# Last expert's rows added on chip, first projection weights loaded ahead of the residual, and block norms in two interleaved steps: one change to a two-block transformer kernel

## The chip, the cores and the metric

The kernel runs on one core of one Trainium2 chip. The metric is the device time of one execution in microseconds (us). Before the change three runs took 2792.95, 2793.12 and 2797.24 us; their median is 2793.12 us.

Engine names as the profile has them: PE is TensorE (PEld its weight loads), DVE is VectorE, ACT is ScalarE, POOL is GpSimd, SP is SyncE (here it only issues DMAs).

## The reference, cut to what matters

Two blocks run on 1024 tokens of width 1024. The first ends in a mixture of 16 experts, each of which takes its own 128 of the tokens; a token that several experts chose gets the sum. The second starts with the norm of that sum, the residual, and another norm in front of a wide projection:

```python
y = einsum('becf,efd->becd', silu(hg) * hu, w_down) * g[..., None]
ff = zeros((t, D_MODEL)).at[idx].add(y)
h = h + g2 * rmsnorm(ff, norm_post_ffn)
u = rmsnorm_2(h, norm_w)
proj = einsum('bsd,de->bse', u, w_in)
```

All of it is float32. The kernel keeps that accuracy by writing a number as a high and a low part in a faster format (fp32r) and forming three products, hi*hi, hi*lo and lo*hi (`mm3`). Products of plain fp32 operands appear as two instructions each in the trace.

## The kernel before

**The experts** (`moe`). Expert weights (16 x 12 MB) are read once, in blocks of 256 x 1024 (1 MB). A block lands in one of six `raw` buffers, ACT casts it to the high part `whi`, DVE subtracts to get the low part `wlo` (`split`, L86 and L87), and PE multiplies (`rows`, L766 to L768). The split parts lie in two rings: `mw` (four buffers) takes four blocks of every six, `ml` (two) the others. Step e of the loop forms the gate product `pg` and the up product `pu` of expert e and the down product `py` of expert e-1. ACT makes silu of `pg` (L717), DVE multiplies it with `pu` into `hh` (L718), PE transposes `hh`, and after `py` ACT scales it into `y` (`combine`, L780). POOL then issues an indirect DMA (L781) that adds the 128 rows of `y` to the array `ff_d` in device memory. All sixteen experts go that way.

**The seam** (`block2`, `ffn_out`). For each of eight blocks of 128 tokens SP loads the residual `h` (L808) and `ff` (L810). ACT squares `ff` and sums (L813), two small ACT steps make 1/rms (`rstd`, L91 and L92), DVE scales `ff` (L815) and adds it to `h` (L816), POOL stores `h` (L75, shown as h_d<-h), ACT squares `h` (L818), two more small steps follow, and DVE forms a diagonal matrix `dg` (L821). After four blocks PE multiplies `h` with `dg`, which transposes and scales at once (L827, 64 products in all), and ACT and DVE write the result as high and low part `uh`, `ul` (L829, L830). Then `hgrn` asks for its first projections: `fill(8)` runs two units of the forget gate, two of the query, four of the value (matmuls L81 to L83), whose weights `wk` loads (L840, two `raw` buffers of 4 KB per partition) and splits.

**What sets the order.** The program is unrolled; a scheduler orders each engine's instructions once, when the program is built, and each engine (and each DMA issuing queue) then takes them in that order. A buffer that lies where an older buffer lay waits for that older one. The pool `pj` of the second block begins where the six expert `raw` buffers lay, so its first buffer, the first `raw` of `wk`, takes the place of the ring's slot 0; the buffers of `ffn_out` lie behind, over the last slots and the buffers of `moe`. There are 192 weight blocks (0 to 191) and ahead of them one load of other weights in slot 0, so block 191 lies in slot 0 at the end.

Of the kernel before, what the change touches and what calls it, by code (L numbers as in the profile page):

```python
# [48 lines left out]
class Kernel:  # L49
# [498 lines left out]
    def phase2(self):  # L548

        nc, I = self.nc, self.I  # L550
        with ExitStack() as st:
# [18 lines left out]
            for i in range(8):  # L570
                if i == 4:
                    ple = self.ple_load(w)
# [110 lines left out]
    def moe(self):  # L683

        with ExitStack() as st:
# [3 lines left out]
            pp = self.pool(st, "moep", 1, space=PSUM)  # L689
            xs = self.chosen(0, w, pp)  # L690
            hh = None
            for e in range(NE + 1):
# [82 lines left out]

    def combine(self, e, w, py):

        y = self.t(w, [P, D], F32, "y", bufs=2)
# [5 lines left out]
    def block2(self):  # L784
        with ExitStack() as st:
            self.stu = ExitStack()
            up = self.pool(self.stu, "uT", side="right")
            self.u = [(self.t(up, [P, KB, 512], F32R, f"uh{g}"), self.t(up, [P, KB, 512], F32R, f"ul{g}")) for g in range(2)]
# [3 lines left out]
            with ExitStack() as st2:  # L792
                self.pp = self.pool(st2, "b2p", 2, space=PSUM)
                self.ffn_out()
                self.hgrn()
            self.fox()

    def ffn_out(self):

        nc, pp = self.nc, self.pp  # L800
        with ExitStack() as st:
            w = self.pool(st, "fo")
            for g in range(2):
                us = []
                for b in range(4):
                    r = slice((g * 4 + b) * P, (g * 4 + b + 1) * P)
                    h = self.t(w, [P, D], F32, "h", bufs=8)
                    nc.sync.dma_start(h, self.h_d[r, :])  # L808
                    ff = self.t(w, [P, D], F32, "ff", bufs=4)
                    nc.sync.dma_start(ff, self.ff_d[r, :])  # L810
                    sq = self.t(w, [P, D], F32, "sq", bufs=2)
                    ss = self.t(w, [P, 2], F32, "ss", bufs=4)
                    nc.scalar.activation(sq, ff, AF.Square, accum_out=ss[:, 0:1])  # L813
                    self.rstd(ss[:, 0:1], D)
                    nc.vector.scalar_tensor_tensor(ff, ff, ss[:, 0:1], self.G2, op0=ALU.mult, op1=ALU.mult)  # L815
                    nc.vector.tensor_tensor(h, h, ff, op=ALU.add)  # L816
                    self.store(self.h2_d[r, :], h)
                    nc.scalar.activation(sq, h, AF.Square, accum_out=ss[:, 1:2])  # L818
                    self.rstd(ss[:, 1:2], D)
                    dg = self.t(w, [P, P], F32, "dg", bufs=8)  # L820
                    nc.vector.tensor_scalar(dg, self.ident, ss[:, 1:2], None, op0=ALU.mult)  # L821
                    us.append((h, dg))
                uh, ul = self.u[g]
                for k in range(KB):
                    tp = self.t(pp, [P, 512], F32, "tp", bufs=2)
                    for b, (h, dg) in enumerate(us):
                        nc.tensor.matmul(tp[:, b * P:(b + 1) * P], h[:, k * P:(k + 1) * P], dg, start=True, stop=True)  # L827
                    nw = self.VC[:, 40 + k:41 + k]
                    nc.scalar.activation(uh[:, k, :], tp, AF.Copy, scale=nw)  # L829
                    nc.vector.scalar_tensor_tensor(ul[:, k, :], tp, nw, f(uh[:, k, :]), op0=ALU.mult, op1=ALU.subtract)  # L830
# [716 lines left out]
```

## Time and profile before

| what | value |
|---|---|
| median of three runs | 2793.12 us |
| the profiled execution: its time, its span | 2797.15 us, 2795.4 us |
| PE busy | 2624.6 us (94%), mean granted clock 0.973 |
| DVE, ACT, POOL busy | 71%, 58%, 12% |
| chain that ended last, shares | PE 77%, ACT 7%, DMA 6%, DVE 6%, issue 4% |
| the experts | about 750 to 1331 us, some 36.4 us for each |
| the seam | 1331 to 1395 us |

The span is the time from the first to the last instruction. In the tables of stretches a column such as "4.58 (x16)" is the engine's busy time and the number of its instructions; PEclk is the granted clock of PE, 1.00 being 2.4 GHz and 0.50 being 1.2 GHz. The chain of waits is read from top to bottom: start, length, what the end of the program was then waiting for.

### The profile page before, as it was taken

The numbers are of one execution on the slowest core, as the hardware profiler recorded it, in microseconds if no ns is written. First come the engines' busy times: TensorE is split into PE (matmuls) and PEld (weight loads), VectorE is DVE, ScalarE is ACT, GpSimd is POOL, SyncE is SP. The second block draws the span as 40 slices with busy tenths as digits, with TensorE's granted clock in tenths as the row PEclk, the third lists the DMA queues.
The fourth block names the chain that finished last, engine by engine and source line by source line (L and its number), as shares of the span: only waits on it lengthen the run. The fifth ranks groups of instructions, "written<-read, shape, count | busy, mean of one in ns | idle before, by whom it ended". The sixth has DMA issues, their size and how long they took to land.

```text
span 2795.4 us, 38785 instructions
## 1 busy us (share of the span) xinstructions
PE 2624.6 (94%) x14237; PEld 2207.7 (79%) x14237; DVE 1998.1 (71%) x3298; ACT 1621.1 (58%) x2858; POOL 328.5 (12%) x499
## 2 busy tenths in 40 slices
PE   8999999899699999999599999999999998989998
PEld 5777888777588877777489999998888897778776
DVE  5965899844698888887557767774777776785535
ACT  4213898743477777776535645553666665674335
POOL 0101000000300000000100000001323232330000
PEclk9999999999799999999799999999999999999999
DMA  7666322255599999998622213325675767466612
GB/s 304 199 232 211 95 84 89 82 186 207 202 380 380 371 372 373 374 360 285 234 55 47 46 46 46 46 54 150 176 187 152 180 165 152 144 188 205 188 61 83
DMA packets 294755, 516.45 MB, mean 185 GB/s; under 512 B 52529, under 2 KB 171902, under 8 KB 293540
## 3 DMA queue, kind: packets, MB, share of 16 engines
q1 hardware_dynamic: 267820, 426.67, 48.9%
q0 software_dynamic: 20608, 65.62, 7.1%
q10 hardware_dynamic: 6136, 21.67, 2.0%
q8 instruction: 113, 1.85, 0.3%
q14 instruction: 78, 0.64, 0.1%
HBM read 421.01 MB, written 92.88 MB: 184 GB/s over the span
## 4 chain that ended last, share of the span: by engine, by line
PE 77%; ACT 7%; DMA 6%; DVE 6%; issue 4%; POOL 1%; SPq 0%; DVEq 0%; POOLq 0%; ACTq 0%
PE mm L81 14%; PE mm L83 13%; PE mm L82 13%; PE av L1345 3%; PE pu L767 2%; PE pu L768 2%; PE pu L766 2%; PE pg L767 2%; PE py L768 2%; PE py L767 2%; PE py L766 2%; PE pg L768 2%; PE sc L1307 2%; PE sc L1057 2%; PE tp L1336 2%
## 5 line engine op out<-in xcount | busy, mean ns | idle before, releaser
L87 DVE TENSOR_TENSOR wlo<-raw,whi 128x2048 fp32r<-128x2048 f32 (+1 forms) x280 | 543.5, 1968 | 172.9 <-ACT whi L86 168.8
L86 ACT CAST whi<-raw 128x2048 fp32r<-128x2048 f32 (+1 forms) x284 | 460.0, 1658 | 133.1 <-PE mm L82 59.6
L81 PE MATMUL mm<-uh,whi 128*128 128x512 f32 x640 | 254.7, 398 | 0.9 <-ACT uh L829 0.9
L82 PE MATMUL mm<-ul,whi 128*128 128x512 f32 x640 | 252.6, 395 | 0.0
L83 PE MATMUL mm<-uh,wlo 128*128 128x512 f32 x640 | 251.9, 394 | 0.0
L81 PE MATMUL mm<-whi,uh 128*128 128x256 f32 x768 | 220.3, 287 | 0.0
L83 PE MATMUL mm<-whi,ul 128*128 128x256 f32 x768 | 220.3, 287 | 0.0
L82 PE MATMUL mm<-wlo,uh 128*128 128x256 f32 x768 | 217.9, 284 | 0.0
L83 PEld LDWEIGHTS mm<-whi,ul 128*128 128x128 f32 x768 | 147.1, 192 | 0.1
L81 PEld LDWEIGHTS mm<-whi,uh 128*128 128x128 f32 x768 | 147.0, 191 | 0.1
L82 PEld LDWEIGHTS mm<-wlo,uh 128*128 128x128 f32 x768 | 146.9, 191 | 0.2
L1314 ACT ACTIVATE lg<-lg,sm 128x128 f32<-128x128 f32 (+7 forms) x128 | 99.4, 777 | 81.8 <-DVE sm L1313 81.3
L450 ACT ACTIVATE e<-sc,mx 128x512 f32<-128x512 f32 (+1 forms) x192 | 118.0, 626 | 40.3 <-DVE mx L449 39.5
L83 PEld LDWEIGHTS mm<-uh,wlo 128*128 128x128 f32 x640 | 120.9, 189 | 23.9
L81 PEld LDWEIGHTS mm<-uh,whi 128*128 128x128 f32 x640 | 121.1, 189 | 22.8 <-ACT uh L829 1.4
L82 PEld LDWEIGHTS mm<-ul,whi 128*128 128x128 f32 x640 | 121.2, 189 | 21.5
L81 PE MATMUL mm<-xh,whi 128*128 128x512 f32 x320 | 127.8, 401 | 2.4 <-DVE stl L87 1.4
L82 PE MATMUL mm<-xl,whi 128*128 128x512 f32 x320 | 127.2, 399 | 0.0
L83 PE MATMUL mm<-xh,wlo 128*128 128x512 f32 x320 | 126.7, 397 | 0.5 <-DVE wlo L87 0.5
L1345 PE MATMUL av<-pT,V 128*128 128x256 f32 x640 | 108.5, 299 | 12.5 <-ACT pT L86 11.1
L1345 PEld LDWEIGHTS av<-pT,V 128*128 128x128 f32 x640 | 91.9, 196 | 35.1 <-ACT pT L86 28.4
L449 DVE TENSOR_REDUCE mx<-sc 128x1 f32<-128x512 f32 (+1 forms) x192 | 110.1, 593 | 7.6 <-PE sc L448 6.8
(399 smaller groups left out, 7054.6 us busy)
## 6 DMA issues: line engine op xcount, KB each, us to landing
raw<-in_w_gate_dram SPq DMA_DIRECT2D x64, 1024.0 KB
raw<-in_w_up_dram SPq DMA_DIRECT2D x64, 1024.0 KB
raw<-in_w_down_dram SPq DMA_DIRECT2D x64, 1024.0 KB
raw<-in_w_in_dram SPq DMA_DIRECT2D x76, 512.0 KB
wada<-in_w_ada_dram SPq DMA_DIRECT2D x32, 512.0 KB
Q<-Q_d SPq DMA_DIRECT2D x64, 256.0 KB
yraw<-yT_d SPq DMA_DIRECT2D x22, 512.0 KB
wa<-in_w_ada_dram SPq DMA_DIRECT2D x8, 1024.0 KB
```

The lines of the kernel that those rows point to most:

```text
L81: self.nc.tensor.matmul(ps, ah, bh, start=(i == 0), stop=False)
L82: self.nc.tensor.matmul(ps, ah, bl, start=False, stop=False)
L83: self.nc.tensor.matmul(ps, al, bh, start=False, stop=(i == n - 1))
L86: self.nc.scalar.copy(hi, src)
L87: (eng or self.nc.vector).tensor_tensor(lo, src, f(hi), op=ALU.subtract)
L449: nc.vector.tensor_reduce(mx[:, m, c:c + 1], ps[:, :n], axis=AX.X, op=ALU.min)
L450: nc.scalar.activation(e[:, c0:c0 + n], ps[:, :n], AF.Exp, scale=-1.0, bias=mx[:, m, c:c + 1], accum_out=sm[:, m, c:c + 1])
L766: self.nc.tensor.matmul(ps[n], xh[:, i, :], hi[:, k, c], start=(i == 0), stop=False)
L767: self.nc.tensor.matmul(ps[n], xh[:, i, :], lo[:, k, c], start=False, stop=False)
L768: self.nc.tensor.matmul(ps[n], xl[:, i, :], hi[:, k, c], start=False, stop=(i == KB - 1))
L1314: nc.scalar.activation(lg[:, :n], lg[:, :n], AF.Exp, scale=-1.0, bias=sm[:, 0:1], accum_out=sm[:, 1:2])
L1345: nc.tensor.matmul(ps[:, :256], V[:, k, :], pT[k // 4][j][:, k % 4, :], start=(k + j == 0), stop=(k == nkb - 1 and j == 1))
```

## The change

The last expert's `combine` goes. Its rows stay on chip as `yh` and `yl` (high and low part), and a matrix `oh` of 0 and 1 (from a loaded row 0..1023 and the token numbers, `places`) says which token each row belongs to. In `ffn_out` PE forms for each block identity x `ff` (plain fp32) plus `oh` x `yh` plus `oh` x `yl` in PSUM. ACT squares and DVE scales from PSUM. The norm of a block is in three functions (`first`, `second`, `third`), and the second half of block b follows the first half of block b+1 on ACT. All sixteen loads are written ahead of the norms, each with its own buffer. The first two weight loads of the projections stand ahead of them, and all later ones after the last of them (`issue_after`). The ring of expert `raw` buffers is moved by five slots through five buffers that are never written. `hh`, `sl` and `y` have one buffer in place of two. `uh` and `ul` take buffers of the `mw` ring. The first units run as forget 0, query 0, forget 1, query 1.

```diff
@@ phase2
                 if i == 4:
+                    for _ in range(NR - 1):
+                        self.t(self.rawp, [P, 2, D], F32, "raw")
                     ple = self.ple_load(w)
@@ moe
+            self.stl = ExitStack()
+            lp = self.pool(self.stl, "last", side="right")
+            self.yh, self.yl = [self.t(lp, [P, D], F32R, x) for x in ("yh", "yl")]
+            self.oh = self.t(lp, [P, SEQ], F32R, "oh")
+            self.ix = self.t(lp, [P, 1], F32, "ix")
...
-                    hh = self.t(w, [P, D], F32, "hh", bufs=2)
+                    hh = self.t(w, [P, D], F32, "hh", bufs=1)
                     for n in range(2):
-                        sl = self.t(w, [P, 512], F32, "sl", bufs=2)
+                        sl = self.t(w, [P, 512], F32, "sl", bufs=1)
                         self.silu = self.nc.scalar.activation(sl, pg[n], AF.Silu)
                         self.nc.vector.tensor_tensor(hh[:, n * 512:(n + 1) * 512], sl, pu[n], op=ALU.mult)
-                if e:
+                if e == NE - 1:
+                    self.places(e, w)
+                if e == NE:
+                    gate = self.gT[:, e - 1:e]
+                    for n in range(2):
+                        c = slice(n * 512, (n + 1) * 512)
+                        self.nc.scalar.activation(self.yh[:, c], py[n], AF.Copy, scale=gate)
+                        self.nc.vector.scalar_tensor_tensor(self.yl[:, c], py[n], gate, f(self.yh[:, c]), op0=ALU.mult, op1=ALU.subtract)
+                elif e:
                     self.combine(e - 1, w, py)
-        self.stx.close()
+        self.stu = self.stx
+    def places(self, e, w):
+        nc = self.nc
+        at = self.t(w, [P, D], F32, "xs", bufs=2)
+        nc.sync.dma_start(at, rowbc(self.I["k_iota"]))
+        nc.vector.tensor_copy(self.ix, self.idxT[:, e:e + 1])
+        nc.vector.tensor_scalar(self.oh, at, self.ix, None, op0=ALU.is_equal)
@@ combine
-        y = self.t(w, [P, D], F32, "y", bufs=2)
+        y = self.t(w, [P, D], F32, "y", bufs=1)
@@ block2
-            self.u = [(self.t(up, [P, KB, 512], F32R, f"uh{g}"), self.t(up, [P, KB, 512], F32R, f"ul{g}")) for g in range(2)]
+            self.u = [[[self.t(self.mw, [P, 4, 512], F32R, n) for _ in range(2)] for n in ("whi", "wlo")] for g in range(2)]
...
+                self.lastin = None
+                self.firstw = [self.wk(c0, P) for c0 in (D, 0)]
                 self.ffn_out()
+                self.stl.close()
+                self.pq = self.pool(st2, "b2q", 2, space=PSUM)
                 self.hgrn()
@@ ffn_out
+            pp = self.pool(st, "fop", 1, space=PSUM)
+            sq = self.t(w, [P, D], F32, "sq")
+            hs, ffs = {}, {}
+            def load(to, src, b):
+                to[b] = self.t(w, [P, D], F32, f"in{b // 4}", bufs=8)
+                self.lastin = nc.sync.dma_start(to[b], src[b * P:(b + 1) * P, :])
+            for b in range(4):
+                load(hs, self.h_d, b)
+            for b in range(4):
+                load(ffs, self.ff_d, b)
+            for b in range(4, 8):
+                load(ffs, self.ff_d, b)
+                load(hs, self.h_d, b)
+            def first(b):
...
+                if b in (1, 3):
+                    pss = [(self.t(self.pp, [P, 512], F32, "mm", bufs=3), n * 512, 512) for n in range(2)]
+                else:
+                    pss = [(self.t(pp, [P, D], F32, "ff"), 0, D)]
...
+                for i, (ps, c0, n) in enumerate(pss):
+                    for k in range(0, n, 512):
+                        o, c = ps[:, k:k + 512], slice(c0 + k, c0 + k + 512)
+                        nc.tensor.matmul(o, self.ident, ff[:, c], start=True, stop=False)
+                        nc.tensor.matmul(o, self.oh[:, r], self.yh[:, c], start=False, stop=False)
+                        nc.tensor.matmul(o, self.oh[:, r], self.yl[:, c], start=False, stop=True)
+                    self.sqa = nc.scalar.activation(sq[:, c0:c0 + n], ps, AF.Square, accum_out=ss[:, 2 * i:2 * i + 1])
+            def second(b):
...
+                self.rstd(ss[:, 0:1], D)
+                for ps, c0, n in pss:
+                    nc.vector.scalar_tensor_tensor(ff[:, c0:c0 + n], ps, ss[:, 0:1], self.G2[:, c0:c0 + n], op0=ALU.mult, op1=ALU.mult)
+                nc.vector.tensor_tensor(h, h, ff, op=ALU.add)
+                self.store(self.h2_d[r, :], h)
+            def third(b):
+                pss, dg, ss = state[b]
+                with self.tc.issue_after(self.sqa.ins):
+                    nc.scalar.activation(sq, hs[b], AF.Square, accum_out=ss[:, 1:2])
+                self.rstd(ss[:, 1:2], D)
+                nc.vector.tensor_scalar(dg, self.ident, ss[:, 1:2], None, op0=ALU.mult)
             for g in range(2):
...
+                blks = list(range(g * 4, g * 4 + 4))
+                first(blks[0])
+                second(blks[0])
+                for b in blks:
+                    if b < blks[-1]:
+                        first(b + 1)
+                        second(b + 1)
+                    third(b)
@@ wk
-            nc.sync.dma_start(raw, self.I["w_in_2"][0, r * P:(r + nk) * P, c0:c0 + n].rearrange("(k p) c -> p k c", p=P))
+            with ExitStack() as st:
+                if self.lastin is not None:
+                    st.enter_context(self.tc.issue_after(self.lastin.ins))
+                nc.sync.dma_start(raw, self.I["w_in_2"][0, r * P:(r + nk) * P, c0:c0 + n].rearrange("(k p) c -> p k c", p=P))
@@ hgrn
+            first = [self.jobs.pop(0)[2] for _ in range(2)]
+            self.ready = [(first[j][g], self.firstw[j]) for g in range(2) for j in range(2)]
             self.fill(8)
```

The products of the heads (`sc`, `o`) get a PSUM pool of their own, opened after `ffn_out`.

## Rows read from the trace of the kernel before

**Rows 1.** Stretches around the seam: busy time (instructions) by engine, granted clock, DMA
```profile
1331.00:1355.00 24.00, 0.00 (x0) 0.00 (x0) 7.55 (x7) 9.28 (x19) 2.14 (x2) 0.60 0.91 273
1355.00:1367.00 12.00, 4.58 (x16) 3.71 (x16) 9.28 (x11) 9.96 (x28) 2.19 (x4) 0.50 1.02 405
...
1395.00:1420.00 25.00, 25.00 (x162) 22.85 (x161) 12.93 (x26) 10.27 (x20) 5.66 (x9) 1.00 0.46 126
```

**Rows 2.** The chain of waits through the seam: start us, us, what
```profile
1331.65 10.29 DMA ff_d<-y,idxT
1342.01 5.58 DMA ff<-ff_d
1347.67 1.16 ACT sq L813 x2
...
1366.91 0.68 ACT uh L829
...
1368.43 3.77 PE tp L827 x16
...
1374.17 1.80 PE tp L827 x16
...
1395.48 0.23 PE mm L82
```

**Rows 3.** One stretch, the instructions on tile mm alone (PE's are first)
```profile
1367.00:1395.00 28.00, 12.95 (x42) 8.12 (x43) 0.00 (x0) 0.51 (x1) 0.89 0.38 144
```

**Rows 4.** SP in order of time, 1296 to 1350
```profile
1327.03 11.33 SPq L840 DMA_DIRECT2D raw<-in_w_in_dram  x3
1338.45 0.55 SPq L808 DMA_DIRECT2D h<-h_d  x1
1342.01 0.34 SPq L810 DMA_DIRECT2D ff<-ff_d  x1
```

**Rows 5.** Groups of instructions, 1331 to 1440: count, busy us, mean ns, idle before, releaser
```profile
L827 PE MATMUL tp<-dg,h 128*128 128x128 f32 x128 | 20.9, 319 | 32.8 <-DVE dg L821 32.8
...
L830 DVE SCALAR_TENSOR_TENSOR ul<-tp,VC,uh 128x512 fp32r<-128x512 f32 x16 | 11.6, 747 | 7.6 <-ACT uh L829 7.3
L829 ACT ACTIVATE uh<-tp,VC 128x512 fp32r<-128x512 f32 x16 | 10.8, 686 | 7.0 <-PE tp L827 6.9
L815 DVE SCALAR_TENSOR_TENSOR ff<-ff,ss,G 128x1024 f32<-128x1024 f32 x8 | 10.2, 1279 | 5.3 <-ACT ss L92 5.3
L816 DVE TENSOR_TENSOR h<-h,ff 128x1024 f32<-128x1024 f32 x8 | 9.8, 1221 | 0.1
...
L91 ACT ACTIVATE ss<-ss,epsc 128x1 f32<-128x1 f32 x16 | 4.4, 288 | 0.2
...
L92 ACT ACTIVATE ss<-ss 128x1 f32<-128x1 f32 x16 | 3.0, 196 | 0.2
```

**Rows 6.** The chain of waits near the start, at full clock: plain fp32 products of 512 columns
```profile
26.04 7.82 PE mm L207 x18
```

**Rows 7.** The chain of waits in the last expert's gate and up products
```profile
1294.14 1.28 ACT L1473
1295.43 1.93 ACT whi L86
1297.38 2.30 DVE wlo L87
```

**Rows 8.** All engines in order of time, 1327 to 1350
```profile
1324.72 2.29 DVE L87 TENSOR_TENSOR wlo<-raw,whi 128x2048 fp32r<-128x2048 f32 x1
...
1330.26 0.39 PE L768 MATMUL py<-whi,htl 128*128 128x512 f32 x1
```

**Rows 9.** ACT within one expert's step, in order of time
```profile
1131.54 0.69 ACT L780 ACTIVATE y<-py,gT 128x512 f32<-128x512 f32 x1 [7.43 <-PE py L768]
```

**Rows 10.** DVE within the same step, in order of time
```profile
1119.72 1.37 DVE L718 TENSOR_TENSOR hh<-sl,pu 128x512 f32<-128x512 f32 x2 [1.07 <-PE pu L768]
```

**Rows 11.** The stretch of one expert: busy time by engine, clock, DMA share, GB/s
```profile
1108.00:1144.00 36.00, 34.56 (x160) 28.27 (x159) 30.08 (x19) 26.31 (x20) 3.15 (x2) 1.00 1.01 375
```

More of the change, by code (lines that the diff above doesn't have):

```diff
@@ L798, in ffn_out @@
     def ffn_out(self):
-        nc, pp = self.nc, self.pp
+        nc = self.nc
         with ExitStack() as st:
             w = self.pool(st, "fo")
-            for g in range(2):
[L804 to L823, printed above, removed]
@@ new lines, in ffn_out @@
+            state = {}
+            def first(b):
+                r = slice(b * P, (b + 1) * P)
+                ff = ffs[b]
+                if b in (1, 3):
+                    pss = [(self.t(self.pp, [P, 512], F32, "mm", bufs=3), n * 512, 512) for n in range(2)]
+                else:
+                    pss = [(self.t(pp, [P, D], F32, "ff"), 0, D)]
+                dg = self.t(w, [P, P], F32, "dg", bufs=8)
+                ss = self.t(w, [P, 4], F32, "ss", bufs=4)
+                for i, (ps, c0, n) in enumerate(pss):
[5 more added lines that the diff above has]
+                    self.sqa = nc.scalar.activation(sq[:, c0:c0 + n], ps, AF.Square, accum_out=ss[:, 2 * i:2 * i + 1])
+                state[b] = (pss, dg, ss)
@@ new lines, in second @@
+            def second(b):
+                r = slice(b * P, (b + 1) * P)
+                h, ff = hs[b], ffs[b]
+                pss, dg, ss = state[b]
+                if len(pss) > 1:
+                    nc.vector.tensor_tensor(ss[:, 0:1], ss[:, 0:1], ss[:, 2:3], op=ALU.add)
+                self.rstd(ss[:, 0:1], D)
[3 more added lines that the diff above has]
+                self.store(self.h2_d[r, :], h)
@@ L824, in ffn_out @@
                 for k in range(KB):
-                    tp = self.t(pp, [P, 512], F32, "tp", bufs=2)
-                    for b, (h, dg) in enumerate(us):
-                        nc.tensor.matmul(tp[:, b * P:(b + 1) * P], h[:, k * P:(k + 1) * P], dg, start=True, stop=True)
+                    uh, ul = self.uk(g, k)
+                    tp = self.t(self.pp, [P, 512], F32, "tp", bufs=2)
+                    for i, b in enumerate(blks):
+                        nc.tensor.matmul(tp[:, i * P:(i + 1) * P], hs[b][:, k * P:(k + 1) * P], state[b][1], start=True, stop=True)
@@ L828, in ffn_out @@
                     nw = self.VC[:, 40 + k:41 + k]
-                    nc.scalar.activation(uh[:, k, :], tp, AF.Copy, scale=nw)
-                    nc.vector.scalar_tensor_tensor(ul[:, k, :], tp, nw, f(uh[:, k, :]), op0=ALU.mult, op1=ALU.subtract)
+                    nc.scalar.activation(uh, tp, AF.Copy, scale=nw)
+                    nc.vector.scalar_tensor_tensor(ul, tp, nw, f(uh), op0=ALU.mult, op1=ALU.subtract)
     def wk(self, c0, n):
@@ L866, in prep, with uk @@
             self.ready += [(u, ws) for u in units]
+    def uk(self, g, k, c=slice(None)):
+        return [x[k // 4][:, k % 4, c] for x in self.u[g]]
     def chan(self, ws, g, m=P):
         ps = self.t(self.pp, [P, 512], F32, "mm", bufs=self.nmm)
-        x = self.u[g]
-        self.mm3(ps[:m, :], [(ws[k], (x[0][:, k, :], x[1][:, k, :])) for k in range(KB)])
+        self.mm3(ps[:m, :], [(ws[k], self.uk(g, k)) for k in range(KB)])
         return ps
@@ L878, in toks @@
         for j in range(2):
-            x, t0 = self.u[(b + j) // 4], ((b + j) % 4) * P
-            self.mm3(ps[:, j * 256:(j + 1) * 256], [((x[0][:, k, t0:t0 + P], x[1][:, k, t0:t0 + P]), ws[k]) for k in range(KB)])
+            g, t0 = (b + j) // 4, ((b + j) % 4) * P
+            self.mm3(ps[:, j * 256:(j + 1) * 256], [(self.uk(g, k, slice(t0, t0 + P)), ws[k]) for k in range(KB)])
         return ps.rearrange("p (b c) -> p b c", b=2)
@@ L1053, in product @@
         def product(lv, half, halves, cols, kl, ql):
-            ps = self.t(pp, [P, 512], F32, "sc", bufs=2)
+            ps = self.t(self.pq, [P, 512], F32, "sc", bufs=2)
             pair = lambda ap, c: ap.rearrange("p (a c j) -> p a c j", a=2, c=4)[:, :, c, :]
@@ L1076, in hgrn_head @@
         for c0 in range(0, 8, 4):
-            ps = self.t(pp, [P, 512], F32, "sc", bufs=2)
+            ps = self.t(self.pq, [P, 512], F32, "sc", bufs=2)
             for c in range(4):
@@ L1107, in hgrn_head @@
             n = min(4, 7 - c0)
-            ps = self.t(pp, [P, 512], F32, "sc", bufs=2)
+            ps = self.t(self.pq, [P, 512], F32, "sc", bufs=2)
             for c in range(n):
@@ L1125, in hgrn_head @@
         for c0 in range(0, 8, 4):
-            ps = self.t(pp, [P, 512], F32, "o", bufs=1)
+            ps = self.t(self.pq, [P, 512], F32, "o", bufs=1)
             for c in range(4):
@@ L1517, in shape_constants @@
         "k_ident": np.eye(P, dtype=np.float32),
+        "k_iota": np.arange(SEQ, dtype=np.float32)[None, :],
         "k_cos": np.ascontiguousarray(np.concatenate([cos, cos], 0)),
```

3 lines of the change are left out of this document (1 added, 2 removed).

## The prediction

> **What bounds the kernel now.** I read the stretches first. In the experts the DMA engines are never free (share 1.01, 375 GB/s) while PE works 34.6 of 36 us [rows 11]: both are near their limit, ACT and DVE are not. After the experts PE does nothing for 24 us and little for 12 more, at half clock, and from 1395 it is never idle again [rows 1]. So time can be won between 1331 and 1395, and what PE does later only moves with it.
>
> The chain of waits through this seam says what PE is waiting for. The last product ends at 1330.65 [rows 8]; the last expert's scatter-add takes 10.29 us until it has landed, the first `ff` load behind it 5.58, then the first square starts at 1347.67 and the first `uh` comes at 1366.91 [rows 2]. SP shows a second obstacle: three weight loads stand ahead of the first `h` load and hold SP from 1327.03 to 1338 [rows 4]; the third needs a buffer of the first, which must land and be split.
>
> I count what PE has to do in those 64.4 us (1330.65 to 1395). It is 64 transposing products, 128 instructions, 16 of which take 1.80 at full clock [rows 2, 5], so 14.4 us, and 42 projection products [rows 3] of 0.23 [rows 2], 9.6 us. That is 24.0 us of work, and **40.4 us are lost**. The rest of the text asks what is lost afterwards.
>
> **The change part by part.**
>
> *Work added to PE.* Each block gets two plain fp32 products of 512 columns and four fp32r ones. Eighteen instructions of the plain kind take 7.82 us [rows 6], 0.434 each, two for a product; the fp32r ones take 0.23. So a block costs 4 x 0.434 + 4 x 0.23 = 2.66 us, eight cost 21.2. PE's work in the seam becomes 45.2 us.
>
> *Scatter-add removed.* The 10.29 us leave the chain. In their place ACT writes `yh` as it wrote `y` and DVE writes `yl`, two instructions of the kind of `ul`, 0.75 each [rows 5]: the last ends about 1.5 us after the last product, at 1332.2. `oh` is a DVE instruction of the size of L816, 1.22 us; its cover is DVE's time between the last split (ends 1327.0) and the last product [rows 8]. Without that cover it costs 0 to 1.2 us. Its source is one DMA on SP behind the last expert weights.
>
> By the row this transfer is worth 10.29 us. The Trainium skill, "DMA: Bandwidth & Descriptors", section "Anatomy of one DMA - SWDGE (gpsimd) path", fits about 2.0 us plus bytes over 436 GB/s for a DMA issued there, which would be an estimate of 3.2 us for these 512 KB; the gain below would then shrink by 7 us and turn into a small loss. The row times the very transfer that goes, so I take the row.
>
> *Loads.* With the ring moved by five, slot 0 holds block 186 at the end and slot 5 block 191. The first two weight loads therefore start when 186 is split, well before 1327, and the third no longer stands ahead of the residual. The first two `h` buffers now lie on slot 5: they wait for the last split, at 1327.0 [rows 8]. SP issues four `h` loads, then four `ff` loads; the scatter-add of the last expert but one, on which `ff` waits, is long out by then if it takes what the last one took. The nearest row for a load is the first `ff`, 5.58 us with others in flight [rows 2]. Four loads of 512 KB ahead at the 405 GB/s of [rows 1] are 1.3 us each. From 1327.0, some 2 us for four issues at 0.55 [rows 4], and about 6.6 us for five loads one behind the other: the first `ff` lands near **1335.6**. Bounds: 1330, if the loads whose buffers are free earlier are put ahead, to 1340, if all wait for the last product. PE then loses 5.0 us (0 to 9) before its first block. The stores stay on POOL, whose queue has lost an indirect DMA.
>
> *First four blocks.* ACT per block has two squares of 1.16 [rows 2] and four small steps of 0.29 and 0.20 [rows 5], 3.3 us, 4 with hand-overs. The first square to the first `uh` took 19.2 us before [rows 2]; now first half and second half interleave and I work out 18: one rung of 1.16 + 0.5 + 1.28 + 1.22 + 1.16 + 0.5 us, three more at 4, a transpose. In these 18 us PE has blocks 1 to 3 (8.0), the first of the second four (2.7) and early transposes (1.8): 12.5 us of work, **5.5 lost** (4 to 8).
>
> *Second four blocks.* All use one PSUM tile of two banks, so a block's products wait until DVE has read the block before: a rung is 1.16 + 0.5 + 1.28 + 2.66 and some 0.5 for hand-overs, 6.1 us, four rungs 24.4, then 2.5 for the last second half. PE's filling is the first transposes (7.2), two units that need only the first half (24 products each, 11.0; before, one) and the remaining blocks (8.0): 26.2 us. The rest of the loss is the eight groups of `uh`, `ul` (0.69 and 0.75 [rows 5]) against 0.9 of transposes each. Together **5 lost** (2 to 8).
>
> *Tail of the experts.* ACT loads a function table behind the last silu, 1.28 us, then casts, DVE splits, and PE waits on that [rows 7]. With one `sl` buffer the second silu comes only after the first `hh` product, and the table load with it, out of this path: 1.3 us won. Bounds: the casts of the first weights may stand in front of the last blocks' (each 128x1024, half of the 1.93 and 2.30 of [rows 7]), 2 us lost; or 2 won.
>
> *Edits at nothing.* One `y` and one `hh` buffer: the earlier content is read one step (36 us) before, and even the slowest scatter-add shown takes 10.29. The new order of the units and the PSUM pool of the heads: PE has filled time after 1395 [rows 1]. One `sl` buffer in the other experts: ACT then waits for the first `hh` product (0.69 [rows 10]), but stands idle 7.43 us later in the same step [rows 9].
>
> *Sum.* 45.2 of work and 5.0 + 5.5 + 5 lost are 60.7 us against 64.4: 3.7 won, and 1.3 in the tail, **5.0 us**. The sum is made in the profiled execution (2797.15, span 2795.4), 4.0 above the median of the runs; I take the difference off the median: 2793.1 - 5.0 = **2788.1**.
>
> **The rivals.**
>
> *Loads come early* (chance 0.14). If the scheduler puts the loads with free buffers first, `ff` is there when `yl` is: 1.5 lost in place of 5.0, and 4 and 3 on the ladders. 53.7 us, with the tail a gain of 12: 2781. For it: nothing in [rows 4] but program order forbids it. Against: there the first `h` load came late.
>
> *PE falls to half clock and stays there* (0.18). At 0.50 the clock is granted when PE is busy 4.58 of 12 us [rows 1], and the same 16 instructions take 3.77 in place of 1.80 [rows 2]. The new blocks come in groups with waits between them. If the first four run at 1.2 GHz, the first costs 2.7 more and each further rung 5.3 in place of 4, 6.6 in all, and the gain is eaten: 2794. The Trainium skill, "TensorE: Matmul & The Clock Gate", section "A second HAM failure mode: psum-queue depth-cycling", describes this: short waits for PSUM between groups throw the clock back again and again. The rows agree that sparse groups here ran at half clock; none shows groups as dense as the new ones, 2.7 of 4 us. The same time comes out if the ring shift does not free the weight buffers early, so that they again load ahead of the residual.
>
> *Slower through ScalarE in every expert* (0.13). With one `sl` buffer the second silu waits on ACT until the up product is done, and the casts of the next weight blocks are queued behind it; DVE's second `hh` product and the splits follow late. Per expert that is at most about 0.69 + 0.69 us on the way to PE; 15 times, 20 us, less the 5 won: 2808. For it: PE has only 1.4 us to spare in 36 [rows 11]. Against: the wait of 7.43 us shows ACT ahead of PE [rows 9]. It decides as soon as a cast behind the silu is the one that PE is waiting for.
>
> **How the numbers follow.** Runs of this kernel scatter by about 0.15%, so 0.2% (5.6 us) is what can be told from no change. My forecast has 0.55, with a range of its own from 2780 to 2793 by the bounds above, not all at once: 0.33 of it lies below 2787.5, 0.22 within. Early loads are faster, 0.14. Half clock is the same, 0.16, or slower, 0.02. ScalarE is slower, 0.13. Faster 0.47, same 0.38, slower 0.15. The range is 2778 to 2798: it takes in the early loads and the half clock and leaves out the third rival and the far ends of the bounds.
>
> **What would show it.** Right: no scatter-add after 1320, the first weight casts before the last product, first `h` load near the end of the last split, first square 9 to 10 us after the last product, first `uh` near 28 after it, PE gapless from 61 us after it. Wrong: a first square before 5 us or after 13; clock 0.50 through the first four blocks; PE waiting in the second four for more than 5; or the step of one expert longer than 36.4 us, which would make all of the seam beside the point.

## The result, and the profile after

The change makes the kernel **slower**: 2816.8 us, median of four runs (2812.9 to 2821.6), against 2795.2 for the kernel before beside them (2793.0 to 2798.0). The ratio is 1.0073, 95% interval 1.0061 to 1.0085; 2788.1 was predicted, with a range from 2778 to 2798. The profiled execution took 2818.0 us with a span of 2816.2, 20.8 more than before.

Four marks divide the two spans: the first gate product, the last expert product, and the first scores of head 0 (the first product on `sc` behind the seam).

| stretch | before, us | after, us | difference |
|---|---|---|---|
| start to first gate product | 750.2 | 751.1 | +0.9 |
| experts, to the end of the last product | 580.5 | 575.8 | -4.7 |
| last product to first scores | 111.2 | 129.6 | +18.4 |
| first scores to the end | 1353.5 | 1359.7 | +6.2 |

So the experts gained, and the seam lost much more than that. The third stretch in one row of the table of stretches, for the kernel before and after (columns as in [rows 1]: us, busy time and instructions of PE, PEld, DVE, ACT, POOL; granted clock, DMA share, GB/s):

```profile
1330.65:1441.86 111.21, 77.47 (x468) 64.17 (x469) 54.17 (x75) 53.81 (x114) 12.83 (x19) 0.83 0.55 178
```
```profile
1326.85:1456.48 129.63, 100.76 (x533) 76.07 (x532) 58.82 (x81) 54.34 (x118) 11.14 (x18) 0.87 0.45 149
```

PE has 23.3 us more to do and its idle time falls only from 33.7 to 28.9. Where the 28.9 lie, the waits of PE in the kernel after show (us in total, times, longest):

```profile
PE ff L858 <- DMA in<-ff_d: 17.7, 1, 17.7
PE tp L896 <- DVE dg L881: 8.5, 3, 3.8
PE ff L858 <- DVE in L872: 2.0, 1, 2.0
```

One wait of **17.7 us for the first `ff`** makes up most of it, where 5.0 had been predicted. The chain of waits of the kernel after leads to it (start us, us, what):

```profile
1321.00 0.66 DVE oh L797
1321.66 2.21 DVE wlo L87
1323.89 0.37 SPq L912
...
1324.93 2.98 SPq L834
...
1328.01 2.05 SPq L834
1330.11 2.06 SPq L834
...
1332.22 2.26 SPq L834
...
1334.53 9.89 DMA in<-ff_d
...
1344.55 2.04 PE ff L858 x2
```

The weight loads (L912) start at 1323.89, where the last split ends (1321.66 + 2.21 and a hand-over). They stand ahead of the residual and need what the last split frees: just as before ([rows 4], 1327.03 behind a split that ended at 1327.01). The four `h` issues behind them (L834) take 2 us each in place of 0.55 [rows 4], so the first `ff` is issued only at 1334.53, and it lands 9.89 us later, among the loads issued before it. While the `h` loads are being issued, from 1325 to 1334.5, the DMA engines are busy for 0.70 of the time and move 185 GB/s:

```profile
1325.00:1334.50 9.50, 1.85 (x9) 1.20 (x7) 1.61 (x3) 2.35 (x3) 0.00 (x0) 0.70 0.70 185
1334.50:1344.40 9.90, 0.00 (x0) 0.00 (x0) 2.25 (x2) 1.04 (x1) 0.00 (x0) 0.50 0.97 342
```

The other stretches of the kernel after, which answer to [rows 1]:

```profile
1344.50:1350.00 5.50, 5.45 (x9) 2.89 (x10) 0.00 (x0) 0.20 (x1) 0.00 (x0) 0.56 1.03 422
1350.00:1367.00 17.00, 12.25 (x44) 7.07 (x42) 11.79 (x16) 12.46 (x35) 2.26 (x4) 0.98 0.69 269
1367.00:1395.00 28.00, 25.75 (x122) 19.27 (x123) 13.71 (x18) 15.02 (x36) 1.60 (x3) 0.89 0.33 114
1395.00:1407.00 12.00, 7.83 (x33) 6.07 (x32) 6.10 (x6) 4.32 (x12) 3.48 (x5) 0.73 0.11 45
1407.00:1430.00 23.00, 23.00 (x153) 21.05 (x152) 15.08 (x29) 11.66 (x20) 3.19 (x5) 0.99 0.33 89
```

The first block runs at half clock (0.56), as does part of 1395 to 1407, behind a wait of 3.8 us. At half clock the first block's eight instructions last from 1344.55 to 1349.76, 5.2 us; one at full clock (the last) takes 2.9.

### The profile page after: what moved, and what is told of

It is laid out like the page before. It is cut to its first block, busy times and chain, and to the rows that moved or that the text cites. A ratio compares the mean times of both kernels' runs of the same rounds, so it can differ in the third digit from the quotient of the medians.

```text
span 2816.2 us, 38971 instructions
## 1 busy us (share of the span) xinstructions
PE 2645.6 (94%) x14301; PEld 2218.0 (79%) x14301; DVE 2005.9 (71%) x3306; ACT 1619.7 (58%) x2862; POOL 326.0 (12%) x498
## 4 chain that ended last, share of the span: by engine, by line
PE 58%; ACT 5%; issue 3%; DVE 3%; DMA 3%; POOL 1%; SPq 0%; DVEq 0%; POOLq 0%; ACTq 0%
PE mm L81 10%; PE mm L82 10%; PE mm L83 10%; PE av L1423 3%; PE pu L783 2%; PE pu L782 2%; PE pu L781 2%; PE pg L782 2%; PE sc L1385 2%; PE pg L783 2%; PE py L783 2%; PE py L782 2%; PE py L781 2%; PE tp L1414 2%; PE sc L1135 2%
## 5 line engine op out<-in xcount | busy, mean ns | idle before, releaser
L86 ACT CAST whi<-raw 128x2048 fp32r<-128x2048 f32 (+1 forms) x284 | 459.4, 1656 | 121.8 <-PE mm L82 60.0
L81 PE MATMUL mm<-whi,whi 128*128 128x256 f32 (+1 forms) x1408 | 476.7, 339 | 1.5 <-ACT yo L1223 0.8
L83 PE MATMUL mm<-whi,wlo 128*128 128x256 f32 (+1 forms) x1408 | 472.9, 336 | 0.0
L82 PE MATMUL mm<-wlo,whi 128*128 128x256 f32 (+1 forms) x1408 | 470.9, 334 | 0.0
L83 PEld LDWEIGHTS mm<-whi,wlo 128*128 128x128 f32 x1408 | 268.5, 191 | 24.3
L81 PEld LDWEIGHTS mm<-whi,whi 128*128 128x128 f32 x1408 | 268.8, 191 | 24.0 <-ACT whi L898 1.3
L82 PEld LDWEIGHTS mm<-wlo,whi 128*128 128x128 f32 x1408 | 268.6, 191 | 21.7
L450 ACT ACTIVATE e<-sc,mx 128x512 f32<-128x512 f32 (+1 forms) x192 | 117.8, 624 | 40.4 <-DVE mx L449 39.6
L782 PE MATMUL pg<-wlo,xsh 128*128 128x512 f32 x256 | 101.3, 396 | 10.0 <-DVE wlo L87 10.0
L87 DVE TENSOR_TENSOR pT<-tp,pT 128x512 fp32r<-128x512 f32 (+1 forms) x192 | 102.2, 549 | 10.3 <-ACT pT L86 9.4
L1385 PE MATMUL sc<-K,Q 128*128 128x512 f32 (+2 forms) x384 | 101.0, 374 | 6.1 <-DVE lg L1390 6.1
L781 PE MATMUL pg<-whi,xsh 128*128 128x512 f32 x256 | 99.2, 399 | 4.9 <-ACT whi L86 3.8
```

The lines of the kernel that those rows point to most:

```text
L81: self.nc.tensor.matmul(ps, ah, bh, start=(i == 0), stop=False)
L82: self.nc.tensor.matmul(ps, ah, bl, start=False, stop=False)
L83: self.nc.tensor.matmul(ps, al, bh, start=False, stop=(i == n - 1))
L86: self.nc.scalar.copy(hi, src)
L87: (eng or self.nc.vector).tensor_tensor(lo, src, f(hi), op=ALU.subtract)
L450: nc.scalar.activation(e[:, c0:c0 + n], ps[:, :n], AF.Exp, scale=-1.0, bias=mx[:, m, c:c + 1], accum_out=sm[:, m, c:c + 1])
```

## The experiments

Three theories stood against each other. **Entry**: the seam begins late, because the ring was not moved and the slow weight loads go ahead of the residual. **Ladder**: the products added to PE, and the PSUM they hold, are the price wherever the loads are. **Expert**: the single buffers of `hh`, `sl` and `y` cost something in each expert. The kernel before took 2797 to 2799 us beside these runs, and 2795 beside the change, so ratios are compared; 0.1% is 2.8 us. All kernels compute the whole reference.

**Run 1, the ring really moved.** No instruction of the change touches its five extra buffers.

```diff
 for _ in range(NR - 1):
-    self.t(self.rawp, [P, 2, D], F32, "raw")
+    self.nc.gpsimd.memset(self.t(self.rawp, [P, 2, D], F32, "raw")[0:1, 0, 0:1], 0.0)
```

> Each of the five extra ring buffers gets one element written by GpSimd, so that the ring is really moved by five slots. Entry theory (the loss of the change lies where the seam begins: the two weight loads wait for the last split, and the residual waits behind them): the first weight loads are issued before 1315 in place of 1323.9, the first ff lands 5 to 9 us after the last product in place of 17.6, and the time falls 8 to 12 us below that of the change, to 2805 to 2809 us. Ladder theory (the price is the products added to TensorE and the PSUM they hold, wherever the loads are): the first ff is early, but the time stays within 4 us of the change's, 2813 to 2821. Expert theory (single buffers of silu cost something in every expert): the step of an expert and the time stay as with the change.

Measured: 2801.7 us, ratio 1.0022 (1.0012 to 1.0031), by the ratios some 14 us below the change. SP in order of time, PE's waits, and the third stretch of this run:

```profile
1305.36 3.09 SPq L912 DMA_DIRECT2D raw<-in_w_in_dram  x2
1316.66 1.76 SPq L834 DMA_DIRECT2D in<-h_d  x4
1321.83 2.79 SPq L834 DMA_DIRECT2D in<-ff_d  x5
```
```profile
PE ff L858 <- DMA in<-ff_d: 5.4, 1, 5.4
```
```profile
1322.49:1438.96 116.47, 99.83 (x533) 75.45 (x532) 58.58 (x81) 54.17 (x118) 11.19 (x18) 0.93 0.43 146
```

The weights are issued at 1305.36, 17.1 us ahead of the last product instead of 3.0, and the wait for `ff` falls from 17.7 to 5.4. Touching the buffers is the only difference, so in the change the five untouched buffers had taken no place in the ring. The other waits of PE are the same to 0.1 us. Entry holds; but this run is still 0.22% slower than before, so entry is not all. What is left of the wait has another cause, as the chain of waits shows:

```profile
1310.10 11.72 DMA ff_d<-y,idxT
1321.83 5.92 DMA in<-ff_d
```

The first `ff` load waits for the scatter-add of the last expert but one, which here runs beside the early weight loads and takes 11.72 us.

**Run 2, the residual ahead of the weights**, with the ring as in the change.

```diff
-                self.firstw = [self.wk(c0, P) for c0 in (D, 0)]
                 self.ffn_out()
 ...
+            self.firstw = [self.wk(c0, P) for c0 in (D, 0)]
             state = {}
```

> The two weight loads stand behind the residual's sixteen loads instead of ahead of them; all else is as in the change. Entry theory: the first ff lands within 5 us of the last product (17.6 with the change) and TensorE starts its first block 10 to 15 us sooner; the first projections start no later than with the change, as their weights have 20 us and more to come in; time 2802 to 2807 us, 10 to 15 below the change. Ladder theory: the blocks start sooner but the end of the seam moves by less than 4 us, 2813 to 2821 us. Expert theory: no difference, 2816 us.

Measured: 2801.6 us, ratio 1.0017 (1.0008 to 1.0027). PE waits only 1.0 us for its first block, but a later wait grows: 8.3 us in one piece, against 3.3 at that place with the change. The chain of waits says for what:

```profile
1324.47 4.57 DMA in<-h_d
1329.06 19.39 DMA raw<-in_w_in_dram
1348.47 1.04 ACT whi L86
1349.52 1.06 ACT sq L879 x2
```

The cast of the late weights (L86) stands in ACT's queue ahead of a square of the norms (L879) and holds it up. The entry theory expected 10 to 15 us and the profile shows 13.6 of 18.4 won back; the weights are now what comes late.

**Run 3, VectorE in place of the identity product.** Loads as in the change.

```diff
-                        nc.tensor.matmul(o, self.ident, ff[:, c], start=True, stop=False)
-                        nc.tensor.matmul(o, self.oh[:, r], self.yh[:, c], start=False, stop=False)
+                        nc.tensor.matmul(o, self.oh[:, r], self.yh[:, c], start=True, stop=False)
 ...
-                    self.sqa = nc.scalar.activation(sq[:, c0:c0 + n], ps, AF.Square, accum_out=ss[:, 2 * i:2 * i + 1])
+                    nc.vector.tensor_tensor(ff[:, c0:c0 + n], ff[:, c0:c0 + n], ps, op=ALU.add)
+                self.sqa = nc.scalar.activation(sq, ff, AF.Square, accum_out=ss[:, 0:1])
```

> The identity product is taken off TensorE: PSUM holds only the last expert's rows, VectorE adds them to ff in place, ScalarE squares ff from its own buffer. The loads stay as in the change. This removes 8 x 4 x 0.434 = 13.9 us of TensorE's work and frees PSUM after one VectorE step of about 1.3 us. Entry theory: the first ff still lands 17 to 18 us after the last product; of the 13.9 us half comes back, 2807 to 2812 us. Ladder theory: all of it and the stalls of the second four blocks come back, 14 to 20 us, 2797 to 2803. Expert theory: what TensorE saves is won but the 18 us lost in the experts stay, 2803 to 2812.

Measured: 2800.9 us, ratio 1.0011 (1.0002 to 1.0020). PE's longest waits and the third stretch:

```profile
PE ff L858 <- DVE in L860: 20.0, 4, 16.3
PE tp L893 <- DVE dg L878: 5.8, 3, 2.2
```
```profile
1326.30:1442.09 115.79, 87.28 (x500) 69.26 (x500) 67.16 (x87) 54.23 (x114) 11.19 (x18) 0.87 0.50 167
```

The entry wait is still there (16.3 us in one piece, now behind DVE's addition, which waits for `ff`), and PE's idle time is what it was, 28.5. PE has 13.5 us less to do, and all of that is won: 13.8 us of the stretch. The entry theory had expected half, the ladder theory all of it and some stalls besides; the time lies in the ladder theory's range. So PE's added work is a price of its own, beside the entry.

**Run 4, the single buffers alone**, in the kernel before.

```diff
-                    hh = self.t(w, [P, D], F32, "hh", bufs=2)
+                    hh = self.t(w, [P, D], F32, "hh", bufs=1)
 ...
-                        sl = self.t(w, [P, 512], F32, "sl", bufs=2)
+                        sl = self.t(w, [P, 512], F32, "sl", bufs=1)
 ...
-        y = self.t(w, [P, D], F32, "y", bufs=2)
+        y = self.t(w, [P, D], F32, "y", bufs=1)
```

> The kernel before with one buffer for each of hh, sl and y, and nothing else of the change. Expert theory: the step of an expert grows from 36.4 by 0.7 to 1.4 us and the time by 10 to 20 us, to 2805 to 2815. Entry and ladder theories: ScalarE's wait for the first hh product shows (about 2.6 us in each expert) but the step stays within 0.1 us of 36.45, and the time within 3 us of the kernel before.

Measured: 2793.4 us, ratio 0.9988 (0.9979 to 0.9997): a little faster. ACT in the last expert's gate and up products, in order of time (in brackets the idle time before, and its releaser):

```profile
1285.66 0.60 ACT L717 ACTIVATE sl<-pg 128x512 f32<-128x512 f32 x1 [2.54 <-PE pg L768]
1286.15 7.34 ACT L86 CAST whi<-raw 128x2048 fp32r<-128x2048 f32 x4
1297.32 0.60 ACT L717 ACTIVATE sl<-pg 128x512 f32<-128x512 f32 x1 [3.83 <-DVE hh L718]
1297.94 1.28 ACT L1473 ACT_TABLE_LOAD   x1
1299.23 3.72 ACT L86 CAST whi<-raw 128x2048 fp32r<-128x2048 f32 x2
```

ACT does wait for the `hh` product, 3.83 us, but it has cast four weight blocks first, and the steps of the down product in the middle of the experts stay at 36.5 us. The last of these steps falls from 38.8 to 36.5 us, since the table load of [rows 7] is now behind those casts, and the first step of the gate product from 28.2 to 25.8; what shortens that one isn't shown. The experts take 576.4 us in place of 580.5: the expert theory falls, with the sign turned round.

**Run 5, the edits of runs 2 and 3 together.**

```diff
+            self.firstw = [self.wk(c0, P) for c0 in (D, 0)]
             state = {}
 ...
+                    nc.vector.tensor_tensor(ff[:, c0:c0 + n], ff[:, c0:c0 + n], ps, op=ALU.add)
```

> The edits of the second and the third run together: the residual ahead of the weight loads, and VectorE instead of the identity product adding ff. If the entry and TensorE's added work are two separate costs, each of about 15 us, they nearly add up: the way from the last product to the first head's scores (129.6 us with the change, 116.0 and 115.8 with one edit each) falls to 103 to 108 us and the time to 2788 to 2794. If they are one cost seen twice (the same idle time is filled by either), it stays at 113 to 117 us and 2799 to 2803.

Measured: 2787.8 us, ratio **0.9962** (0.9948 to 0.9975), the lowest of all runs, below both kernels. The third stretch is 27.6 us shorter than with the change (13.6 and 13.8 with one edit each):

```profile
1325.40:1427.39 101.99, 87.09 (x501) 69.80 (x501) 65.76 (x87) 53.98 (x114) 11.26 (x18) 0.92 0.49 155
```

Two costs, then, that add up.

**Run 6, the edits of runs 1 and 3 together.**

```diff
+    self.nc.gpsimd.memset(self.t(self.rawp, [P, 2, D], F32, "raw")[0:1, 0, 0:1], 0.0)
 ...
+                    nc.vector.tensor_tensor(ff[:, c0:c0 + n], ff[:, c0:c0 + n], ps, op=ALU.add)
```

> The moved ring (first run) and VectorE instead of the identity product (third run) together. Two separate costs: 102 to 108 us from the last product to the first scores, and 2787 to 2794 us; better than the fifth run by up to 4 us, since the weights are split before the norms and ScalarE doesn't wait for them between two squares. One cost seen twice: 113 to 117 us, 2798 to 2803. If VectorE, with one more step of about 1.2 us per block, becomes what the first four blocks wait for, the first uh comes later than the 29.8 us after the last product of the first run, 32 to 34.

Measured: 2788.3 us, ratio 0.9971 (0.9961 to 0.9981); 102.8 us in the stretch, first `uh` 27.8 us behind the last product. The same as run 5 within the intervals, by the other way of clearing the entry.

**Run 7, the identity product in the first four blocks only.**

```diff
+                        if b < 4:
+                            nc.tensor.matmul(o, self.ident, ff[:, c], start=True, stop=False)
 ...
+                    if b >= 4:
+                        nc.vector.tensor_tensor(ff[:, c0:c0 + n], ff[:, c0:c0 + n], ps, op=ALU.add)
```

> As the sixth run, but the identity product stays in the first four blocks, where TensorE waits anyway, and VectorE adds in the second four only, where TensorE has the transposes and the first projections to do. If TensorE's work counts only where it has no idle time, this is as good as the sixth run or better, by 0 to 4 us; if VectorE isn't the limit in the first four blocks, it is 3 to 6 us slower than the sixth (four identity products of 1.74 us more).

Measured: 2794.3 us, ratio 0.9990 (0.9980 to 1.0001). Some 5 us behind run 6, and 109.4 us in the stretch: products in the first four blocks are not free although PE has idle time there. The first square comes 9.9 us behind the last product in place of 5.8, because a block's products now start only when `ff` is there, and at half clock.

**Run 8, the scatter-add kept**, the rest as in run 1.

```diff
-                if e == NE - 1:
-                    self.places(e, w)
-                if e == NE:
 ...
-                elif e:
+                if e:
                     self.combine(e - 1, w, py)
 ...
+                pss = [(ff, 0, D)]
```

> As the first run (moved ring), but the last expert's rows go out with the scatter-add as before the change, and no products are formed in the norms; ScalarE squares ff from its own buffer. This undoes the on-chip addition alone. If it pays (10.3 us of transfer against products that fit into idle time), this run is 4 to 10 us slower than the first run, 2806 to 2812. If it costs more than it brings (21 us of products against the transfer of 10 us and a load of 6), this run is 5 to 12 us faster than the first, 2790 to 2797 us, with the first square 16 to 18 us after the last product as in the kernel before.

Measured: 2792.3 us, ratio 0.9985 (0.9976 to 0.9994), 0.37% faster than run 1. Its chain of waits:

```profile
1323.40 6.39 DMA ff_d<-y,idxT
1329.81 3.21 DMA in<-ff_d
...
1333.05 1.16 ACT sq L845 x2
```

The first square was expected at 16 to 18 us behind the last product and comes at 10.6. **The scatter-add takes 6.39 us, not the 10.29 of [rows 2]**, and the load behind it 3.21, not 5.58, now that no weight load is issued beside them. So the addition on chip, as the change does it, costs about 10 us more than the transfer that it saves. Done as in run 6, with VectorE in place of the identity product, it does not: run 6 is some 4 us below this run, with a stretch of 102.8 us against 109.3, though the two intervals overlap a little.

**Run 9, the edits of runs 1, 2 and 3 together.**

```diff
+    self.nc.gpsimd.memset(self.t(self.rawp, [P, 2, D], F32, "raw")[0:1, 0, 0:1], 0.0)
 ...
+            self.firstw = [self.wk(c0, P) for c0 in (D, 0)]
 ...
+                    nc.vector.tensor_tensor(ff[:, c0:c0 + n], ff[:, c0:c0 + n], ps, op=ALU.add)
```

> The moved ring, the residual ahead of the weights, and VectorE's addition, all three: a candidate for the best. If the late weights still held ScalarE in the fifth run, they now come earlier and it gains 1 to 4 us on the fifth run: 99 to 102 us from the last product to the first scores, 2784 to 2788 us. If the two entry edits remove the same wait, it is the same as the fifth run within 2 us, 2786 to 2790.

Measured: 2793.4 us, ratio 0.9979 (0.9968 to 0.9991), and 106.9 us in the stretch: a miss. With the ring moved, the first `h` loads are issued at 1318.02 in place of 1306.07 in run 5, and the weights behind the residual at 1332.92 in place of 1329.12. So the weights are on the chain of waits for longer than in run 2, and hold a cast until 1354.4:

```profile
1323.88 10.27 DMA in<-h_d
1334.17 20.25 DMA raw<-in_w_in_dram
1354.44 1.05 ACT whi L86
```

**Run 10, TensorE kept busy**, in run 5.

```diff
+                if b < 4:
+                    dm = self.t(pp, [P, 512], F32, "dm")
+                    for _ in range(8):
+                        nc.tensor.matmul(dm, self.oh[:, r], self.yh[:, 0:512], start=True, stop=True)
```

> The fifth run with eight products of 128x512 (0.23 us each at full clock) into a PSUM tile that nobody reads, behind each of the first four blocks' products, to keep TensorE at full clock through the first four blocks. If half clock there costs (the rival of the prediction), the first transposes and projections run at full clock and the first scores come 2 to 5 us earlier than in the fifth run, 2783 to 2786 us. If ScalarE and VectorE set the pace there and TensorE only waits, nothing is won: 2786 to 2791 us, the first uh at 25 us after the last product as in the fifth run.

Measured: 2794.2 us, ratio 0.9982 (0.9973 to 0.9992). It decides nothing: from 1335 to 1350 the granted clock is 0.74 in place of 0.61, and the first `uh` comes at 31.8 us, later, not sooner; but the chain of waits here also passes through a weight load that lands at 1361.4 and holds ScalarE, so that the part of the added products can't be told from that of the loads.

**Run 11, the loads alone**, in the kernel of run 4.

```diff
-                    nc.sync.dma_start(ff, self.ff_d[r, :])
+                    self.lastin = nc.sync.dma_start(ff, self.ff_d[r, :]) if g * 4 + b < 4 else (nc.sync.dma_start(ff, self.ff_d[r, :]), self.lastin)[1]
 ...
+            with self.tc.issue_after(self.lastin.ins):
```

> The kernel before with one buffer for each of hh, sl and y (fourth run) and with all weight loads of the projections behind the residual's loads, as the only change to the seam; the scatter-add and the norms stay as they were. If the weight loads ahead of the residual were a cost of their own in the kernel before, the scatter-add and the first ff land sooner than 16 us after the last product, the first square comes 4 to 6 us earlier than the 16.8 us of the fourth run, and the time is 2787 to 2790 us. If the scatter-add's own 10.3 us end last whatever SP does, the first square stays at 16 to 17 us and the time within 2 us of the fourth run, 2791.5 to 2795.5. If the weights then come too late, it is slower than the fourth run by 2 to 6 us.

Measured: 2796.1 us, ratio 0.9990 (0.9980 to 0.9999), no gain on run 4. Both halves of the expectation are in its chain of waits:

```profile
1321.67 6.61 DMA ff_d<-y,idxT
...
1329.26 5.75 DMA ff<-ff_d
1335.10 1.15 ACT sq L813 x2
...
1347.64 15.38 DMA raw<-in_w_in_dram
1363.04 1.05 ACT whi L86
```

The scatter-add is again short (6.61, against 10.37 in run 4) and the first square comes at 11.0 us in place of 16.8. Then the weights come late, at 1363, and hold the first projection, where PE waits 4.6 us; the stretch is 112.7 us against 110.3 in run 4.

**Run 12, TensorE kept busy**, in run 6.

```diff
+                if b < 4:
+                    dm = self.t(pp, [P, 512], F32, "dm")
+                    for _ in range(8):
+                        nc.tensor.matmul(dm, self.oh[:, r], self.yh[:, 0:512], start=True, stop=True)
```

> The eight unread products per block again, for the first four blocks, now in the sixth run, where the weights are on chip early and no cast waits for them among the norms (that wait spoilt the tenth run). TensorE's granted clock from the first block to the fourth, 0.58 in the sixth run, should rise to 0.8 or more. If half clock is a price there, the first uh comes before the 27.8 us after the last product of the sixth run and the first scores by 2 to 5 us before its 102.8: 2783 to 2786 us. If ScalarE and VectorE set the pace in the first four blocks, the first uh stays at 27 to 29 us and the time within 2 us of the sixth run, 2786 to 2791.

Measured: 2795.0 us, ratio 0.9986 (0.9976 to 0.9996), slower than run 6 and outside both expectations, with 106.1 us from the last product to the first scores. The stretch of the first blocks in run 6, and in this run:

```profile
1329.00:1350.00 21.00, 12.16 (x34) 8.21 (x34) 17.55 (x21) 14.46 (x37) 2.25 (x4) 0.58 0.95 356
```
```profile
1329.00:1350.00 21.00, 15.06 (x59) 11.22 (x58) 16.63 (x19) 10.75 (x28) 1.73 (x3) 0.81 1.00 384
```

The clock rises from 0.58 to 0.81 as it should, and the first `uh` comes at 30.6 us, not sooner than the 27.8 of run 6: the added products stand in the way of the next block's (the first product of the third block comes 10.9 us behind the last expert product, 5.8 in run 6). So no gain from the higher clock shows, but the run doesn't show either that half clock is free there. DVE is busy 17.6 of 21 us in run 6, which speaks for DVE setting the pace; neither run 10 nor this one decides it. For the change itself, where PE's products stand between `ff` and the square, the question stays open too.

## Why the prediction was wrong

The forecast made the lost time of the seam 5.0 + 5.5 + 5 = 15.5 us beside 45.2 of work. Counted the same way from the table above, the change lost 64.4 + 18.4 - 45.2 = 37.6.

- **The step "Loads" failed.** It said that the first weight loads start well before 1327 because the ring is moved by five, so that the first `ff` costs PE 5.0 us. The ring had not moved, the loads started at the last split, and PE waited 17.7: 12.7 us of the miss. Run 1, with the ring moved, gives 5.4, a first square 10.2 us behind the last product and a first `uh` 29.8 behind it (5.0, 9 to 10 and 28 in the forecast; 17.7, 22.9 and 42.9 with the change). The prediction did name this failure, and the late first square as its sign, but priced it at 6 us, beside the clock's rival: it left out that the weights hold up the residual's issue and its transfer too. Nor was the scatter-add of the last expert but one "long out by then": in run 1 it lands at 1321.83, only 0.7 us ahead of the last product, and the first `ff` load waits for it.
- **Work was priced at full clock, and slow work counted as lost time.** PE's other idle time in the seam is 28.9 - 17.7 = 11.2 us, where 5.5 + 5 had been predicted: the two ladders were right in sum. But 37.6 - 28.9 = **8.7 us** are products that ran slower than priced, most of them at half clock; the forecast had none. In run 1 the same three terms are 5.4, 11.2 and 7.8 us. Little of the 8.7 is new, as PE's waits in the kernel before show:

```profile
PE tp L827 <- DVE dg L821: 32.8, 5, 24.6
PE mm L81 <- ACT uh L829: 0.9, 2, 0.6
```

Of the 40.4 us that the prediction called lost, PE waited only 33.7. The other 6.6 were products: they took 30.6 us in place of the 24.0 priced, at half clock until 1373, and the forecast let these 6.6 us vanish without saying why. The change added 23.3 us of busy time where 21.2 had been priced, so 2.1 of the 8.7 are its own. The rival of half clock did not come as described: it had the first four blocks at 1.2 GHz, for 6.6 us, but only the first was (5.2 us in place of 2.9); the stretch from 1350 to 1367 has a granted clock of 0.98. The rung of the second four was forecast at 6.1; the last took 6.9, the two before it 11.3 and 11.5 (products at 1360.2, 1371.5, 1383.0 and 1389.9), with the first transposes and projections among them.

- **The scatter-add's price was a price in company.** The 10.29 us of [rows 2] are right for the kernel before, but they hold some 4 us caused by the weight loads: run 11, which moves only the loads in the kernel of run 4, brings 10.37 down to 6.61, and run 8 has 6.39. The prediction took the row as the transfer's own. The Trainium skill's fit ("DMA: Bandwidth & Descriptors", section "Anatomy of one DMA - SWDGE (gpsimd) path"), 3.2 us by estimate, is still below the 6.39 and 6.61 measured with no projection weights beside it.
- **The tail of the experts** was right in mechanism and too small: 1.3 us forecast, 4.7 won: the last step of the down product 2.2 us shorter, and the first step of the gate product, which the prediction had not looked at, 28.2 us before and 25.2 after. Run 4 has most of it (4.0) from the buffers alone.
- **The rival of ScalarE in every expert** is refuted by run 4. One `y`, `hh` and `sl` buffer cost nothing, as forecast.
- **Nothing was allowed for the time after the seam**, which grew by 6.2 us. PE's order there is the same as before. A part is seen: behind a wait of 2.6 us, shortly before the second attention begins, PE ran at half clock for 6.8 us, while the kernel before had the same wait and kept full clock.

```profile
1953.50:1960.30 6.80, 5.86 (x15) 4.46 (x16) 2.17 (x6) 2.12 (x4) 1.49 (x7) 0.50 0.95 233
```
```profile
1941.00:1948.00 7.00, 7.00 (x33) 5.79 (x32) 0.71 (x2) 0.60 (x1) 2.56 (x9) 1.00 1.00 293
```

By the first softmax of that attention the way is 3.3 us longer. The other 2.9 us came later, and this time scatters from run to run: 1353.6 us in run 8, 1357.6 in run 1, 1366.1 in run 9. What of it belongs to the change stays open.

The sum: -5.0 forecast, +22.1 in the seam (12.7, 0.7 and 8.7), -3.4 in the experts, +6.2 after the seam and +0.9 ahead of the experts give +20.8, the difference of the spans.

## What to carry to other kernels

A buffer shift is only there if the trace shows the load moving: look where the first transfer that should profit is issued, here still at the end of the last split. Work moved from a DMA onto an engine has to be priced in the queue in which it will run, and the transfer it replaces at its price without its neighbours; here 10.3 us of transfer were 6.4, against 23 us more of busy PE. What an engine loses in a stretch is to be split into waiting and slow work: filling the waits does not remove the slow work, and here 6.6 us of the 40.4 were that. And what is put ahead in one queue is put behind in another: in runs 2, 9 and 11 the residual stood ahead of the weights, and the weights' cast then held ScalarE or the first projection.

## What the runs showed of the hardware

- A transfer's time hung on its neighbours: the same scatter-add of 512 KB took 10.29 and 10.37 us with three weight loads issued next to it (before, run 4), 6.39 and 6.61 us without (runs 8 and 11).
- The weight loads have rows of 512 bytes. While two of them and the first `h` loads were in flight the DMA engines were busy 0.70 of the time and moved 185 GB/s, against 375 at a share of 1.01 in the experts [rows 11]. In the packed traces a packet of 512 bytes took 34 ns on average in that stretch, one of 4096 bytes 178 ns in the experts (1110 to 1140). The issue of an `h` load took 2.0 to 3.0 us on SP right behind the weight loads, 0.55 before, and 0.44 in run 1, where they were 11 us ahead. That the short rows are the reason for the slow issue isn't shown.
- After one and the same wait of 2.6 us PE's clock fell to 0.50 in the kernel after and stayed at 1.00 in the kernel before, with PE's products in the same order. What decided it, these runs don't show.
